# One layer's modulation loads after the projections, the other layer's delta rule projected first

## The chip, the cores and the metric

The kernel runs on one core of one Trainium2 chip. The metric is the device time of one execution in microseconds (us), lower is better. A core has a matrix engine (PE, with its weight loads PEld), a vector engine (DVE), a scalar engine (ACT), GpSimd (POOL) and a sync engine (SP); each takes its instructions in order from its own queue. In this kernel every DMA is issued from SP's queue, so an issue that waits holds up all issues behind it.

## The reference

Two layers work on 512 latent tokens and 256 context tokens of width 1024, in f32. In each layer:

```python
mod_l = split(silu(c) @ mod_w[i] + mod_b[i], 6)      # shifts, scales and gates; mod_c the same from c_ctx
h_l = modulate(x, norm_mix_g[i], mod_l[0], mod_l[1])
pa_l, pb_l, pc_l, pd_l = _cumsplit(h_l @ w_in[i], MIXER_IN)
oa = rwkv7_mixer(pa_l, pa_c, ...)            # delta rule, recurrent, both directions
ob = diff_attention_mixer(pb_l, pb_c, ...)   # softmax attention, two maps
oc = gla_mixer(pc_l, pc_c, ...)              # gated linear attention, chunks of 64
od = gqa_mixer(pd_l, pd_c, ...)              # softmax attention
x = x + mod_l[2] * (concatenate([oa, ob, oc, od]) @ w_out[i])
x = x + mod_l[5] * conv_ffn(modulate(x, norm_ffn_g[i], mod_l[3], mod_l[4]), ...)
```

The second layer computes outputs for the latent tokens alone. Parts 0 and 1 of the modulation are wanted before the projections, part 2 first in the output projection, parts 3 and 4 in the second norm.

## The kernel before

Each layer has a mixing stage and then a feed-forward stage. The mixing stage is written as generators that `weave` interleaves by costs that they yield: `rwkv` (the delta rule), `gla`, `attentions` (the differential attention in two halves and then the grouped-query one), `projections`, and in the first layer `mod_mix`. That order of writing, tile reuse and a reordering at build time fix each engine's queue before the run.

`projections` multiplies the normed tokens by blocks of `w_in`: `win_feat` (L754) gives features by tokens, `win_tok` (L762) tokens by features in tiles of 128 tokens, 24 matmuls each (L770). `weights` (L367) loads a block, ACT casts it to a high part (L382) and POOL subtracts to get the low part (L383). Before the change the order of blocks in both layers is: GLA's q, k, v, r; the delta rule's k, v, r, w, a, g; the differential attention's k, v, q; the grouped-query kv and q. Three flags release the other streams: "gla ready", "rw g" and so on, "da ready" and "gq ready".

The delta rule then computes for each direction `features` (L1417, with L1424 on PE and L1443 on DVE), `blocks` (L1465 on PE, which reads L1443's result), the `bonus` (L1547, which reads L1454 of POOL), and `inverses`: 31 steps of two DVE instructions (L1492 and L1494), each step reading the one before. After the inverses come, chunk by chunk, `rw_prep` (L1620 on PE) and `rw_chain` (L1738, L1743). The attention first prepares its keys (`rope`, then `split_stack` with L937 on DVE, then PE transposes at L432), then runs scores (L1012), a maximum (L1018, DVE), an exponential (L1020, ACT) and values.

`mod_first` computes eight pairs of modulation blocks before the first norm. `mod_mix` (L521) computes the other twelve of the first layer beside the mixing stage: per pair 1 MB of weights, eight small matmuls (L470), a copy (L472, ACT), two matmuls that wait for that copy (L474), and an add (L477). It takes one of PSUM banks 0 to 3, which the projections and the attention use too. The second layer's modulation runs on DVE in the feed-forward stage and is not touched.

Of the kernel before, what the change touches and what calls it, by code (L numbers as in the profile page):

```python
# [15 lines left out]
AF = mybir.ActivationFunctionType  # L16
ALU = mybir.AluOpType
# [4 lines left out]
P = 128  # L22
# [201 lines left out]
class Net:  # L224
# [7 lines left out]
    RB = ((4, 8), (4, 8))  # L232

# [287 lines left out]
    def mod_mix(self, dt):  # L521

        ws = [self.new([4, 256]) for _ in range(3)]
        e = 0
        for i in range(KD, len(MODP)):
            w = []
            for q in range(2):
                self.nc.sync.dma_start(out=ws[e % 3], in_=self.A["modp"][i][:, 4 * q:4 * q + 4])
                w += [ws[e % 3][:, k] for k in range(4)]
                e += 1  # L530
            ps = yield from self.bank(1, 0, 4)
            self.mod_pair(i, w, ps)
            self.free(ps)
            yield dt
        self.free(*ws, self.c32)
# [240 lines left out]
    def projections(self, li, h, S):  # L776
# [6 lines left out]
        h2 = [[a[:, e] for a in h] for e in range(2)]  # L783

        G = S["gla"] = {"q": self.new([T]), "k": self.new([T])}
        yield from self.win_feat(li, "glaq", qs, h2, lambda ps: nc.scalar.mul(out=G["q"][:, :nq], in_=ps[:, :nq], mul=32 ** -0.5), 8)
        yield from self.win_feat(li, "glak", both, h2, lambda ps: nc.scalar.copy(out=G["k"], in_=ps[:, :T]), 8)
        G["v"], G["g"] = self.new([NT, 256]), self.new([NT, 32])

        def ev(t, ps):  # L790
            nc.scalar.copy(out=G["v"][:, t], in_=ps[:, :256])
            nc.vector.tensor_copy(out=G["g"][:, t], in_=ps[:, 256:288])

        yield from self.win_tok(li, "glav", range(NT), h2, ev)
        G["r"] = self.new([NT, 256])

        def evr(t, ps):
            th = self.new([256])
            nc.scalar.activation(out=th, in_=ps[:, :256], func=AF.Tanh, scale=0.5)
            nc.vector.scalar_tensor_tensor(out=G["r"][:, t], in0=th, scalar=1.0, in1=ps[:, :256], op0=ALU.add, op1=ALU.mult)  # L800
            self.free(th)

        yield from self.win_tok(li, "glar", qt, h2, evr)
        S["gla ready"] = True

        R = S["rw"] = {}
        c0 = self.small([P, 9], "c0")
        nc.vector.tensor_tensor(out=c0, in0=self.par(li, "mu0", 0, 9), in1=self.par(li, "mu1", 0, 9), op=ALU.add)
        nc.vector.tensor_scalar(out=c0, in0=c0, scalar1=-1.0, scalar2=1.0, op0=ALU.mult, op1=ALU.add)

        def shifted(i, dst, segs):
            def f(ps):
                n = segs[-1][1]
                nc.scalar.activation(out=dst[:, :n], in_=ps[:, :n], func=AF.Copy, scale=c0[:, i:i + 1])
                for a, b in segs:
                    nc.vector.scalar_tensor_tensor(out=dst[:, a + 1:b], in0=ps[:, a:b - 1], scalar=self.par(li, "mu0", i),
                                                   in1=dst[:, a + 1:b], op0=ALU.mult, op1=ALU.add)
                    nc.vector.scalar_tensor_tensor(out=dst[:, a:b - 1], in0=ps[:, a + 1:b], scalar=self.par(li, "mu1", i),
                                                   in1=dst[:, a:b - 1], op0=ALU.mult, op1=ALU.add)
            return f  # L820

        for nm, i0, m, segs in (("k", 2, 2, both), ("v", 4, 2, both), ("r", 0, 2, qs), ("w", 6, 1, both), ("a", 7, 1, both), ("g", 8, 1, qs)):
# [1123 lines left out]
```

## Time and profile before

| | us |
|---|---|
| runs | 2373.57, 2382.31, 2385.05 (median 2382.31) |
| profiled execution | 2371.69, of which the span is 2369.8 |
| PE busy in the span | 2194.0 (93%) |
| first layer: projections, then the rest of its mixing stage | 64 to 391, 391 to 743 |
| second layer: mixing stage | 1392 to 1960 |

The profiled execution is 10.6 us below the median of the runs. Stretches are given in us from the start of the span; their bounds were chosen at the first norm's end, the end of the first layer's projections, the start of the output projection, and in the second layer where PE's idle share changes.

### The profile page before, as it was taken

How to read it: one execution, taken by the hardware profiler on the slowest of the kernel's cores; microseconds unless marked ns; L12 is line 12 of the kernel's file. 1: busy time of each engine (PE TensorE's matmuls, PEld its weight loads, DVE VectorE, ACT ScalarE, POOL GpSimd, SP SyncE). 2: the span in 40 equal slices, each digit the busy share in tenths (PEclk: the TensorE clock that was granted, in tenths of full speed). 3: DMA queues.
4: the chain of work that ended last, by engine and by line, in shares of the span. 5: the costliest groups of instructions: out<-in, count | busy, mean ns of one | idle time of the engine just before them, and what ended most of it. 6: DMA issues, size and time to landing. Idle time of an engine off the chain costs nothing. (4 is left out here: it accounts for less than half of the span.)

```text
span 2369.8 us, 40603 instructions
## 1 busy us (share of the span) xinstructions
PE 2194.0 (93%) x15656; PEld 1852.1 (78%) x15656; DVE 1327.0 (56%) x2900; ACT 934.2 (39%) x1730; POOL 995.9 (42%) x999
## 2 busy tenths in 40 slices
PE   7989996889989999999999989995899979999999
PEld 3877786768768788888888877785778868888888
DVE  3143567878864696765445643378877565332323
ACT  3333222555564422322223443332465544433333
POOL 1433437123422344434434634455443224555556
PEclk7999997889999999999999989997889989999999
DMA  8322354433234243343333521144233242333334
GB/s 324 116 72 82 102 150 108 105 89 93 58 123 143 82 137 116 109 142 106 116 107 107 172 65 55 59 126 132 69 98 87 77 138 72 102 94 99 98 98 134
DMA packets 241265, 258.51 MB, mean 109 GB/s; under 512 B 102896, under 2 KB 186160, under 8 KB 241072
## 3 DMA queue, kind: packets, MB, share of 16 engines
q1 hardware_dynamic: 241072, 255.92, 36.1%
q8 instruction: 123, 2.02, 0.4%
q14 instruction: 70, 0.57, 0.1%
HBM read 209.69 MB, written 37.77 MB: 104 GB/s over the span
## 5 line engine op out<-in xcount | busy, mean ns | idle before, releaser
L392 PE MATMUL pst<-slab,slab 128*128 128x512 f32 (+1 forms) x6552 | 1236.5, 350 | 14.4 <-POOL slab L650 5.8
L392 PEld LDWEIGHTS pst<-slab,slab 128*128 128x128 f32 x6552 | 1049.6, 190 | 195.8 <-issue 11.3
L383 POOL TENSOR_TENSOR slab<-slab,slab 128x512 fp32r<-128x512 f32 (+1 forms) x428 | 563.7, 1326 | 661.1 <-ACT slab L382 621.3
L382 ACT CAST slab<-slab 128x512 fp32r<-128x512 f32 (+1 forms) x428 | 258.7, 612 | 592.3 <-PE pst L392 418.6
L770 PE MATMUL pst<-slab,slab 128*128 128x256 f32 (+1 forms) x1872 | 254.1, 295 | 9.3 <-POOL slab L383 8.0
L770 PEld LDWEIGHTS pst<-slab,slab 128*128 128x128 f32 x1872 | 242.4, 199 | 20.4 <-POOL slab L383 9.5
L432 PE MATMUL pst<-cst,slab 128*128 128x128 f32 (+1 forms) x968 | 166.4, 305 | 69.1 <-DVE slab L937 21.7
L683 DVE SCALAR_TENSOR_TENSOR slab<-pst,pp,slab 128x511 f32<-128x511 f32 x66 | 41.6, 658 | 299.2 <-ACT slab L680 299.2
L432 PEld LDWEIGHTS pst<-cst,slab 128*128 128x128 f32 (+1 forms) x968 | 120.6, 153 | 96.6 <-DVE slab L937 24.3
L1620 PE MATMUL pst<-slab,slab 128*128 128x128 f32 (+4 forms) x1320 | 160.8, 283 | 7.3 <-DVE slab L1646 3.4
L1620 PEld LDWEIGHTS pst<-slab,slab 128*128 128x128 f32 (+3 forms) x1320 | 132.3, 179 | 29.6 <-issue 14.6
L714 DVE SCALAR_TENSOR_TENSOR slab<-pst,fgate,slab 128x512 f32<-128x512 f32 (+1 forms) x144 | 88.2, 628 | 104.9 <-PE pst L392 104.7
L1020 ACT ACTIVATE slab<-pst,mx 128x768 f32<-128x768 f32 (+1 forms) x120 | 97.7, 815 | 67.6 <-DVE mx L1018 64.3
L1018 DVE TENSOR_REDUCE mx<-pst 128x1 f32<-128x768 f32 (+1 forms) x120 | 100.2, 846 | 35.6 <-PE pst L1012 20.1
L695 POOL TENSOR_TENSOR slab<-slab,slab 128x768 fp32r<-128x768 f32 (+1 forms) x44 | 73.9, 1680 | 70.2 <-ACT slab L694 70.2
L551 DVE SCALAR_TENSOR_TENSOR slab<-slab,slab 128x512 bf16<-128x512 f32 x104 | 92.2, 886 | 5.1 <-DMA slab<-in_modw_dram 3.5
L1048 PE MATMUL pst<-slab,slab 128*64 128x128 f32 x832 | 67.0, 290 | 5.0 <-DVE slab L429 2.9
L1031 ACT ACTIVATE slab<-slab,r 128x768 f32<-128x768 f32 (+1 forms) x80 | 67.7, 852 | 10.0 <-DVE r L1030 9.3
L689 ACT ACTIVATE slab<-slab 128x768 f32<-128x768 f32 (+1 forms) x44 | 32.4, 737 | 85.7 <-DVE slab L685 85.6
L694 ACT CAST slab<-slab 128x768 fp32r<-128x768 f32 (+1 forms) x44 | 32.1, 729 | 85.0 <-DVE slab L691 84.9
L1012 PE MATMUL pst<-slab,slab 128*128 128x384 f32 (+1 forms) x144 | 48.8, 407 | 14.0 <-ACT slab L1020 6.4
L1048 PEld LDWEIGHTS pst<-slab,slab 128*64 128x64 f32 x832 | 46.9, 141 | 18.1 <-DVE slab L429 6.3
(320 smaller groups left out, 2626.6 us busy)
## 6 DMA issues: line engine op xcount, KB each, us to landing
slab<-in_wup_dram SPq DMA_DIRECT2D x88, 512.0 KB, 3.7
slab<-in_modw_dram SPq DMA_DIRECT2D x112, 256.0 KB, 3.0
slab<-in_wdn_dram SPq DMA_DIRECT2D x48, 512.0 KB, 3.5
slab<-in_win_dram SPq DMA_DIRECT2D x46, 512.0 KB, 3.9
slab<-in_modp_dram SPq DMA_DIRECT2D x40, 512.0 KB, 7.0
slab<-in_wout_dram SPq DMA_DIRECT2D x16, 512.0 KB, 3.7
slab<-in_xT_dram SPq DMA_DIRECT2D x16, 384.0 KB, 5.3
slab<-kb SPq DMA_DIRECT2D x24, 256.0 KB, 3.0
```

The source lines that it names most:

```text
L382: nc.scalar.copy(out=w[0], in_=st[:, k:k + q])
L383: nc.gpsimd.tensor_tensor(out=w[1], in0=st[:, k:k + q], in1=w[0].bitcast(F32), op=ALU.subtract)
L392: self.nc.tensor.matmul(ps[:, a:b], w[i][k][:, cols], x[j][k][:, a:b], start=(k == 0 and q == 0), stop=(k == nk - 1 and q == 2))
L432: self.nc.tensor.transpose(out, a.bitcast(F32) if a.dtype != F32 else a, self.c["ident"])
L551: self.tc.keep_in_program_order(nc.vector.scalar_tensor_tensor(out=junk, in0=w, scalar=1.0, in1=self.sc[s][e], op0=ALU.mult, op1=ALU.mult, ...
L695: nc.gpsimd.tensor_tensor(out=HL[:, 1, :n], in0=th[:, :n], in1=HL[:, 0, :n].bitcast(F32), op=ALU.subtract)
L714: nc.vector.scalar_tensor_tensor(out=x[m][:, a:b], in0=ps[:, a:b], scalar=gate[:, m, s:s + 1], in1=x[m][:, a:b], op0=ALU.mult, op1=ALU.add)
L770: self.nc.tensor.matmul(ps[:, :n], h[i][k][:, t * P:(t + 1) * P], w[j][k], start=(k == 0 and q == 0), stop=(k == KD - 1 and q == 2))
L1018: nc.vector.tensor_reduce(out=mx, in_=sv, axis=AX.XY, op=ALU.max, negate=True)
L1020: nc.scalar.activation(out=p[m][:, a:].rearrange("p (e c) -> p e c", e=2 - a // hb), in_=sv, func=AF.Exp, bias=mx, accum_out=lsum[:, m:m + 1])
L1048: nc.tensor.matmul(acc[64 * e:64 * e + 64, :P], vs[e][:, i + j], aT[:, 256 * j + P * e:256 * j + P * e + P], start=(first and j == 0), sto ...
L1620: mm = lambda o, a, b, pos: nc.tensor.matmul(o, a, b, start=True, stop=True, tile_position=pos)
```

## The change

Three edits, with everything they pull along through the interleaving:

- `mod_mix` first waits for "gq ready", the last flag of the first layer's projections. Its loads are 48 of 256 KB instead of 24 of 512 KB, into twelve tiles instead of three, and the pairs are yielded every 4000 instead of 16000 cost units.
- In the second layer (`DELTA = (1,)`) the delta rule's blocks are projected before GLA's. In both layers its w and a now come before r and g; `rwkv` waits for all of them before its features.
- The first attention begins when six slabs of the arena are free instead of five.

```diff
+    DELTA = (1,)
-    def mod_mix(self, dt):
-        ws = [self.new([4, 256]) for _ in range(3)]
-        e = 0
+    def mod_mix(self, S, dt):
+        n = 12
+        yield from self.wait(S, "gq ready")
+        ws = [self.new([2, 256]) for _ in range(n)]
         for i in range(KD, len(MODP)):
             w = []
-            for q in range(2):
-                self.nc.sync.dma_start(out=ws[e % 3], in_=self.A["modp"][i][:, 4 * q:4 * q + 4])
-                w += [ws[e % 3][:, k] for k in range(4)]
-                e += 1
+            for q in range(4):
+                t = ws[(4 * i + q) % n]
+                self.nc.sync.dma_start(out=t, in_=self.A["modp"][i][:, 2 * q:2 * q + 2])
+                w += [t[:, k] for k in range(2)]
...
+        def gla(hi):
             G = S["gla"] = {"q": self.new([T]), "k": self.new([T])}
...
+        def delta(hi):
             R = S["rw"] = {}
...
-        for nm, i0, m, segs in (("k", 2, 2, both), ("v", 4, 2, both), ("r", 0, 2, qs), ("w", 6, 1, both), ("a", 7, 1, both), ("g", 8, 1, qs)):
+            for nm, i0, m, segs in (("k", 2, 2, both), ("v", 4, 2, both), ("w", 6, 1, both), ("a", 7, 1, both), ("r", 0, 2, qs), ("g", 8, 1, qs)):
...
+        for i, f in enumerate((delta, gla) if li in self.DELTA else (gla, delta)):
+            yield from f(4 if i else 8)
...
             if before is None:
-                yield from self.room(5)
+                yield from self.room(6)
...
-                streams.append(self.mod_mix(16000))
+                streams.append(self.mod_mix(S, 4000))
```

The counts of instructions are the same on every engine but for the 24 additional loads. What moves is shown at three places. Lines behind the edited functions stand 2 to 7 higher in the changed file: L1492 and L1494 of before are L1499 and L1501 there, L937 is L944, L770 is L773, L1547 is L1554, L1706 is L1713, L1508 to L1510 are L1515 to L1517.

On DVE in the second layer, where the first key is split (L937) among the last inverse steps. Before:

```order
L920 TENSOR_TENSOR slab_322_6989<-slab_322_6989,slab_340_11497 128x128
L1494 TENSOR_TENSOR slab_355_12059<-slab_355_12059,slab_353_11875 96x5x27
L412 SCALAR_TENSOR_TENSOR rs0qda_13664<-rs1qda_13665,rs0qda_13664 128x32
L924 TENSOR_TENSOR slab_322_6989<-slab_322_6989,rs0kda_13154 128x128
L1492 TENSOR_TENSOR slab_353_11875<-slab_353_11875,slab_355_12059 96x112
L920 TENSOR_TENSOR slab_21_169<-slab_21_169 128x128
L1494 TENSOR_TENSOR slab_355_12059<-slab_355_12059,slab_353_11875 96x4x28
L937 TENSOR_TENSOR slab_390_13745<-slab_322_6989,slab_390_13745 128x8x32
```

The changed kernel on the same engine, at the last inverse step of the layer (GLA's gate L1215 to L1231 and the query norms follow it):

```order
L1501 TENSOR_TENSOR slab_18_166<-slab_18_166,slab_373_12000 96x2x30
L1499 TENSOR_TENSOR slab_373_12000<-slab_373_12000,slab_18_166 96x31
L1501 TENSOR_TENSOR slab_18_166<-slab_18_166,slab_373_12000 96x31
L863 TENSOR_REDUCE msqda_13460<-slab_21_169 128x8
L1215 TENSOR_SCALAR slab_33_385<-pst,pp 128x768
L1219 SCALAR_TENSOR_TENSOR slab_118_3789<-reset,slab_33_385 128x768
L863 TENSOR_REDUCE msqda_13460<-slab_368_11840 128x8
L1231 TENSOR_TENSOR slab_324_7081<-slab_118_3789 128x768
```

Counted over the whole queue: before, 34 of the layer's 62 inverse steps stand behind the first key's split and 25 behind the first maximum of the scores; now none does, and the first split stands 75 rows behind the last step.

On PE in the second layer, at the end of the bonus. Before, the keys' transposes follow at once:

```order
L1547 MATMUL pst<-rk_12898,slab_151_4601 128x2
L1547 MATMUL pst<-rk_12898,slab_94_3573 128x2
L432 MATMUL pst<-cst,slab_390_13745 128x128 x12
L770 MATMUL pst<-slab_212_5540,slab_315_6605 128x256
L770 MATMUL pst<-slab_329_7170,slab_315_6605 128x256
```

The changed kernel at the same place:

```order
L1554 MATMUL pst<-rk_12209,slab_382_12218 128x2
L1554 MATMUL pst<-rk_12209,slab_324_7081 128x2
L773 MATMUL pst<-slab_330_7192,slab_334_7209 128x256
L773 MATMUL pst<-slab_331_7196,slab_334_7209 128x256
L773 MATMUL pst<-slab_330_7192,slab_334_7209 128x256
```

Behind the bonus 216 projection matmuls were left before, and 576 are now; when the first score is issued 168 were left, and now none is. In the first layer it is the other way round: none was left behind the first score or the first L1620, and now 142 and 48 are.

On SP in the first layer, where the delta rule's exchanges are issued (L1508 and L1509 load chunks, L1687 and L1706 copy between partitions). Before:

```order
L1505 DMA slab_22_170<-ra_91 128x512
L1508 DMA slab_18_166<-scrout_389 64x4x64
L1706 DMA slab_18_166<-slab_5_100 64x64 x7
L1687 DMA slab_98_3637<-slab_98_3637 64x4x128 x2
L1706 DMA slab_18_166<-slab_5_100 64x64
```

The changed kernel, with the pairs' loads (L532) between the chunk loads and the copies (L1713 and L1694):

```order
L1515 DMA slab_23_171<-scrout_392 64x4x64 x3
L532 DMA slab_16_164<-in_modp_dram 128x512
L532 DMA slab_96_3437<-in_modp_dram 128x512 x2
L976 DMA slab_33_385<-rawdaq 128x128
L532 DMA slab_22_170<-in_modp_dram 128x512
L532 DMA slab_6_101<-in_modp_dram 128x512 x3
L532 DMA slab_7_102<-in_modp_dram 128x512
L1713 DMA slab_22_170<-slab_96_3437 64x64 x4
L532 DMA slab_7_102<-in_modp_dram 128x512 x2
L532 DMA slab_16_164<-in_modp_dram 128x512
L1694 DMA slab_118_3789<-slab_112_3742 64x4x128 x2
```

The 24 loads of `mod_mix` stood among the loads of the projection weights; now 48 stand among these exchanges.

## Rows read from the trace of the kernel before

**Rows 1.** The page: span, busy share of PE, its 40 slices, the granted clock.

```profile
span 2369.8 us, 40603 instructions
...
PE 2194.0 (93%) x15656; PEld 1852.1 (78%) x15656; DVE 1327.0 (56%) x2900; ACT 934.2 (39%) x1730; POOL 995.9 (42%) x999
...
PE   7989996889989999999999989995899979999999
...
PEclk7999997889999999999999989997889989999999
```

**Rows 2.** Stretches: bounds, length, busy us and instructions by engine, clock, DMA.

```profile
core 0: us, PE busy (x) PEld busy (x) DVE busy (x) ACT busy (x) POOL busy (x), PEclk, DMA share, GB/s
64.00:391.00 327.00, 300.85 (x2542) 258.23 (x2541) 147.43 (x335) 99.34 (x176) 137.78 (x138) 0.96 0.35 107
391.00:500.00 109.00, 83.19 (x640) 66.94 (x639) 84.86 (x204) 48.87 (x101) 37.35 (x65) 0.76 0.38 95
500.00:743.00 243.00, 226.86 (x2147) 185.33 (x2148) 179.02 (x476) 145.48 (x318) 73.29 (x115) 0.97 0.37 106
1392.00:1594.00 202.00, 191.22 (x1590) 164.42 (x1588) 94.22 (x187) 76.01 (x130) 95.22 (x84) 0.98 0.27 75
1594.00:1657.00 63.00, 38.15 (x320) 34.31 (x318) 50.58 (x139) 14.77 (x32) 32.83 (x47) 0.78 0.51 140
1657.00:1740.00 83.00, 67.32 (x494) 57.55 (x496) 71.99 (x178) 43.46 (x86) 33.49 (x57) 0.88 0.31 82
1740.00:1924.00 184.00, 178.34 (x1870) 150.68 (x1868) 121.66 (x292) 110.52 (x232) 62.15 (x98) 0.97 0.35 93
1924.00:1960.00 36.00, 23.08 (x164) 18.55 (x161) 16.93 (x58) 10.66 (x20) 6.20 (x7) 0.81 0.36 116
```

**Rows 3.** PE's waits in 1594 to 1740: total us, times, longest.

```profile
PE pst L1465 <- DVE slab L1443: 10.1, 1, 10.1
PE pst L432 <- DVE slab L937: 7.8, 3, 7.1
PE pst L1547 <- POOL slab L1454: 3.1, 1, 3.1
```

**Rows 4.** DVE's queue around L1443 at 1619: start, us, instruction.

```profile
1619.39 0.41 DVE L1492 TENSOR_TENSOR slab<-slab,slab 96x247 f32<-96x247 f32 x1
1619.71 0.95 DVE L1443 TENSOR_TENSOR slab<-slab,slab 128x768 f32<-128x768 f32 x1
1620.58 0.40 DVE L1494 TENSOR_TENSOR slab<-slab,slab 96x247 f32<-96x247 f32 x1
```

**Rows 5.** Stretch 1594 to 1740, L1492 and then L1494 alone: DVE busy.

```profile
1594.00:1740.00 146.00, 26.05 (x62) 0.84 0.40 107
...
1594.00:1740.00 146.00, 25.43 (x62) 0.84 0.40 107
```

**Rows 6.** PE's waits in 64 to 391.

```profile
PE pst L474 <- ACT slab L472: 7.2, 2, 4.3
```

**Rows 7.** PE's waits in 391 to 743.

```profile
PE pst L432 <- DVE slab L937: 13.6, 6, 4.9
```

**Rows 8.** The page: costliest groups, the projections by tokens.

```profile
L770 PE MATMUL pst<-slab,slab 128*128 128x256 f32 (+1 forms) x1872 | 254.1, 295 | 9.3 <-POOL slab L383 8.0
```

**Rows 9.** L1018, first layer and second: durations, first and last start.

```profile
L1018 DVE TENSOR_REDUCE mx<-pst x72: 405/948/959, 419.9 to 719.2; 128x1 f32<-128x768 f32 x48, 128x1 f32<-128x256 f32 x24
...
L1018 DVE TENSOR_REDUCE mx<-pst x48: 939/957/959, 1657.8 to 1925.9; 128x1 f32<-128x768 f32 x48
```

**Rows 10.** Stretch 64 to 391, L470 and then L474 alone: PE, PEld busy.

```profile
64.00:391.00 327.00, 13.61 (x176) 4.92 (x176) 0.96 0.35 107
...
64.00:391.00 327.00, 7.05 (x44) 6.74 (x44) 0.96 0.35 107
```

**Rows 11.** L528 in 64 to 391: issue time in ns, then landing.

```profile
L528 SPq DMA_DIRECT2D slab<-in_modp_dram x19: 327/382/1103, 74.0 to 329.6; - x19
...
DMA to landing us min/median/max: 3.7/5.1/7.4
```

**Rows 12.** The page: DMA issues, size of one, median us to landing.

```profile
slab<-in_modw_dram SPq DMA_DIRECT2D x112, 256.0 KB, 3.0
slab<-in_wdn_dram SPq DMA_DIRECT2D x48, 512.0 KB, 3.5
```

More of the change, by code (lines that the diff above doesn't have):

```diff
@@ L783, in projections @@
         h2 = [[a[:, e] for a in h] for e in range(2)]
[L785 to L820, printed above, removed]
@@ L822, in projections, with ev, evr @@
-        for nm, i0, m, segs in (("k", 2, 2, both), ("v", 4, 2, both), ("r", 0, 2, qs), ("w", 6, 1, both), ("a", 7, 1, both), ("g", 8, 1, qs)):
-            R[nm] = [self.new([T]) for _ in range(m)]
-            for p in range(m):
-                yield from self.win_feat(li, f"rw{i0 + p}", segs, h2, shifted(i0 + p, R[nm][p], segs))
-            S["rw " + nm] = True
+        def gla(hi):
+            G = S["gla"] = {"q": self.new([T]), "k": self.new([T])}
+            yield from self.win_feat(li, "glaq", qs, h2, lambda ps: nc.scalar.mul(out=G["q"][:, :nq], in_=ps[:, :nq], mul=32 ** -0.5), hi)
+            yield from self.win_feat(li, "glak", both, h2, lambda ps: nc.scalar.copy(out=G["k"], in_=ps[:, :T]), hi)
+            G["v"], G["g"] = self.new([NT, 256]), self.new([NT, 32])
+            def ev(t, ps):
+                nc.scalar.copy(out=G["v"][:, t], in_=ps[:, :256])
+                nc.vector.tensor_copy(out=G["g"][:, t], in_=ps[:, 256:288])
+            yield from self.win_tok(li, "glav", range(NT), h2, ev)
+            G["r"] = self.new([NT, 256])
+            def evr(t, ps):
+                th = self.new([256])
+                nc.scalar.activation(out=th, in_=ps[:, :256], func=AF.Tanh, scale=0.5)
+                nc.vector.scalar_tensor_tensor(out=G["r"][:, t], in0=th, scalar=1.0, in1=ps[:, :256], op0=ALU.add, op1=ALU.mult)
+                self.free(th)
+            yield from self.win_tok(li, "glar", qt, h2, evr)
+            S["gla ready"] = True
@@ new lines, in delta, with shifted, f @@
+        def delta(hi):
+            R = S["rw"] = {}
+            c0 = self.small([P, 9], "c0")
+            nc.vector.tensor_tensor(out=c0, in0=self.par(li, "mu0", 0, 9), in1=self.par(li, "mu1", 0, 9), op=ALU.add)
+            nc.vector.tensor_scalar(out=c0, in0=c0, scalar1=-1.0, scalar2=1.0, op0=ALU.mult, op1=ALU.add)
+            def shifted(i, dst, segs):
+                def f(ps):
+                    n = segs[-1][1]
+                    nc.scalar.activation(out=dst[:, :n], in_=ps[:, :n], func=AF.Copy, scale=c0[:, i:i + 1])
+                    for a, b in segs:
+                        nc.vector.scalar_tensor_tensor(out=dst[:, a + 1:b], in0=ps[:, a:b - 1], scalar=self.par(li, "mu0", i),
+                                                       in1=dst[:, a + 1:b], op0=ALU.mult, op1=ALU.add)
+                        nc.vector.scalar_tensor_tensor(out=dst[:, a:b - 1], in0=ps[:, a + 1:b], scalar=self.par(li, "mu1", i),
+                                                       in1=dst[:, a:b - 1], op0=ALU.mult, op1=ALU.add)
+                return f
+            for nm, i0, m, segs in (("k", 2, 2, both), ("v", 4, 2, both), ("w", 6, 1, both), ("a", 7, 1, both), ("r", 0, 2, qs), ("g", 8, 1, qs)):
+                R[nm] = [self.new([T]) for _ in range(m)]
+                for p in range(m):
+                    yield from self.win_feat(li, f"rw{i0 + p}", segs, h2, shifted(i0 + p, R[nm][p], segs), hi if nm == "k" else 4)
+                S["rw " + nm] = True
```

## The prediction

> **What bounds the kernel now.** I read the page first. PE is busy for 2194.0 of 2369.8 us, so the whole kernel can lose at most 176 us of idle time to a better order; PE's slices and the clock's dip at the same places, in the two mixing stages [rows 1]. I then cut those stages into stretches [rows 2]. In the second layer PE is busy 94.7% of 1392 to 1594 and 96.9% of 1740 to 1924, but 105.5 of the 146 us between (38.15 + 67.32 in 63 + 83): 40.5 us are idle there. DVE is the busiest engine in the first of the two pieces, 50.58 of 63 us. PE's waits say why: 10.1 us for L1443, 7.8 us for the first keys' L937, 3.1 us for L1454 [rows 3]. L1443 stands between inverse steps in DVE's queue [rows 4], and those steps take 26.05 + 25.43 = 51.5 us of DVE in this stretch alone [rows 5]. So DVE's long serial loop collides with the second direction's features and with the attention's first keys, while PE has little else queued. In the first layer PE is busy 300.9 of 327 us during the projections (26 idle), 83.2 of 109 behind them (26 idle), 226.9 of 243 after that (16 idle) [rows 2]. The pairs of `mod_mix` lie in the first of these, and the waits for the first keys in the second [rows 6, 7].
>
> **The second layer, part by part.** The new order issues the same instructions, so its worth is in the 40.5 idle us. All 62 inverse steps now stand ahead of the first key's split, and 576 instead of 216 projection matmuls stand behind the bonus. At 254.1/1872 = 0.136 us each [rows 8], 576 are 78 us of PE work, which covers the loop's 51.5 us of DVE. If the 105.5 us of PE work goes through at the 94.7% of the stretch ahead of it, it takes 111 us: -35. The lowest is 0 (the idle time stays), the highest the whole 40.5.
>
> The clock comes on top. It was 0.78 over 63 us and 0.88 over 83 us, against 0.98 ahead [rows 2]: at its two levels (2.4 and 1.2 GHz) that is 0.20x2x63 + 0.10x2x83 = 42 us more at half clock, of which PE was busy 72%, 30 us. Work bound by columns would win 15 of these; small matmuls that wait for weights win less, so I take 8 (bounds 0 and 15). The Trainium skill, "TensorE: Matmul & The Clock Gate", part "What's actually happening", says that the array is throttled by default and that activity releases it; by that alone all 15 would come back, and the sum below would be 7 us lower. The stretch's rows show the clock falling with PE's idle share, but not how much of the work follows it.
>
> Against this stands what the new order cannot cover. The chain from features to blocks is the same length and now has the inverses of the first direction in it still; the keys still need ACT, POOL and DVE before PE can transpose. Of the 21 us of waits named above I leave a third, +7 (bounds 0 and 21). Projecting GLA later costs nothing as long as it ends before the output projection; its cover is the attention, which lasts from 1657 to 1926 [rows 9]. The order of w, a, r and g costs nothing, because the delta rule waits for all of them anyway. Six free slabs instead of five act through the queue's order alone. Second layer: -35 - 8 + 7 = -36.
>
> **The first layer.** The pairs cost PE 13.61 + 7.05 us in the projections' stretch [rows 10], for 11 of the 12, and PE waits 7.2 us for the copy between their two steps [rows 6]. All of this, 28 us, leaves a stretch that PE bounds: -28. The work itself comes back behind it: 20.7x12/11 = 22.5 us. There 42 us of PE are idle (25.8 + 16.1), and half of the work should fall into them: +11 (bounds 0 and 22.5). The copy's wait returns in part: +4 (0 to 10). The first keys' waits of 13.6 us [rows 7] now have projection matmuls between them, 142 behind the first score, 19 us of work: -9 (0 to -13.6). Sum -22. On SP 24 loads become 48; one issue took 0.38 us at the median [rows 11], so 24 more are some 9 us of a queue that is not the bound. The loads bring 12.6 MB into a stretch whose DMA engines are busy 37 to 38% [rows 2]; what that costs is the slower rival below, and 0 in this sum, since they are issued ahead by up to three pairs.
>
> **Sum.** -36 - 22 = -58 against the profiled execution's 2371.7: 2314. That execution was 10.6 us below the median of the runs, 2382.3; the same 58 us off the median gives 2324, and I say 2325. By the bounds the second layer lies between +7 and -55 and the first between +4 and -42; both at the same end are not expected, and for this case alone I give 2295 to 2360. A measurement tells about 0.5%, 12 us, from no change.
>
> **The rivals.** *The attention sets the second layer's end.* Its maxima run from 1657.8 to 1925.9, 268 us [rows 9], and now start behind the last projection matmul. That puts 168 x 0.136 = 23 us more PE work ahead of the first score, as much as the 25 us that PE idles in 1594 to 1657 [rows 2]: the start stays, and if the attention again needs 268 us the stage ends where it did. Then only the first layer gains: 2382 - 22 = 2360. For it: the attention is one serial stream. Against: in the first layer the same stream did 72 maxima in 299 us, 4.2 us each against 5.6 here [rows 9], so it can run faster when PE lets it. Chance 0.15.
>
> *The waits only move.* In the second layer the blocks still wait for L1443, which still stands behind inverse steps, and GLA's chain, now woven into the token projections, waits in the keys' place; in the first layer the 22.5 us of pairs and their 7.2 us of waits come back whole, because the stretch they go to is bound by chains across engines, and every added matmul lengthens one. Both layers then gain nothing: 2382, within 12. For it: DVE was at 78% there too (84.86 of 109) [rows 2]. Chance 0.14.
>
> *The pairs' loads stand in the way of the delta rule.* This is the slower side. SP issues in order, and 16 loads of 256 KB now stand between the chunk loads and the copies that a chunk's PE steps wait for. One such load lands in 3.0 us [rows 12]; if the four of a pair hold up the exchange behind them one after another, that is 12 us for each of 12 pairs, 144 us. With half to two thirds of the pairs in front of an exchange that PE waits for, 72 to 96 us, the time would be 2382 - 58 + 72 = 2396 to 2420. It decides from 58/12 = 4.8 us per pair. For it: the pairs' own loads of 512 KB took 5.1 us at the median beside the projections [rows 11]. Against: the DMA engines moved only 95 GB/s there [rows 2], and a load of 512 KB from another tensor lands in 3.5 us [rows 12], hardly longer than one of half the size, so loads overlap. The Trainium skill, "DMA: Bandwidth & Descriptors", part "Bandwidth", has the rule to batch loads to 1 MiB, and the fit in its part "Anatomy of one DMA" (2.0 us and 436 KB per us, for DMAs issued from POOL) makes a pair 4x2.6 instead of 2x3.2 us if loads go one by one, an estimate of 48 us over 12 pairs; the rows here agree that half a load is far from half as long (3.0 and 3.5 us). Chance 0.13.
>
> **How the numbers follow.** The forecast case keeps 0.58. Faster by over 0.5%: 0.58, and most of the attention's case (0.13) = 0.71. Same: 0.02 of it, 0.12 of the moved waits, and 0.02 of the loads' case = 0.16. Slower: 0.13. The range leaves out the slower rival and the edges: 2292, for a clock and cover at their bounds, to 2376, which takes in the attention's case.
>
> **What would show it.** Right: in the second layer PE busy over 93% in every stretch from the norm to the attention's end, no wait for L1443 (now L1450) above 3 us, the inverses' last step 50 us or more ahead of the first maximum; the output projection 532 instead of 568 us behind the stage's start. In the first layer the projections end near 360, their stretch has no small matmuls, and the next is no longer than before. Wrong: PE waiting for L1713, L1694 or L1515's landings in the first layer; a clock under 0.8 over 50 us or more in the second; or attention maxima that again take 268 us while PE idles.

## The result: slower by 1%

The changed kernel takes 2402.67 us (median of 4 runs, 2396.89 to 2404.17), the kernel before 2378.44 in the runs beside it (2373.57 to 2385.05): ratio 1.0098, 95% interval 1.0073 to 1.0123. The forecast was 2325. The page of the changed kernel (span, PE's busy share, its slices, the granted clock; answers to [rows 1]):

```profile
span 2395.1 us, 40626 instructions
...
PE 2210.8 (92%) x15656; PEld 1859.4 (78%) x15656; DVE 1332.4 (56%) x2900; ACT 935.8 (39%) x1730; POOL 1001.1 (42%) x999
...
PE   6999868899899999999999989788699989999999
...
PEclk8999978799999999999999989879799999999999
```

The span grew by 25.3 us: 16.8 of them are more PE busy time for the same 15656 instructions, 8.5 more idle time. Two marks divide the growth, the moments at which DVE reaches the first product of each output projection (L1822 before, L1829 after). Before they stand at 734.8 and 1956.2 us, now at 748.6 and 1979.8: the first layer's mixing lost 13.8 us, and from the first mark to the second the time went from 1221.4 to 1231.2, +9.8. Neither layer gained. The stretches of the changed kernel follow, in the columns of [rows 2]: the first layer's projections, two pieces behind them, then the second layer's mixing stage.

```profile
61.00:404.00 343.00, 300.76 (x2491) 263.83 (x2490) 179.56 (x397) 113.04 (x200) 158.18 (x164) 0.92 0.30 86
404.00:520.00 116.00, 102.31 (x880) 75.08 (x877) 67.55 (x196) 48.47 (x112) 23.69 (x47) 0.84 0.56 163
520.00:757.00 237.00, 214.58 (x1986) 173.66 (x1986) 160.84 (x428) 133.97 (x286) 69.77 (x108) 0.94 0.36 101
1405.00:1530.00 125.00, 119.35 (x800) 100.82 (x799) 67.73 (x115) 50.13 (x84) 55.76 (x47) 0.97 0.41 113
1530.00:1610.00 80.00, 59.51 (x520) 52.67 (x518) 57.52 (x141) 19.32 (x36) 40.62 (x36) 0.75 0.29 77
1610.00:1697.00 87.00, 79.24 (x758) 70.88 (x756) 32.73 (x95) 21.26 (x41) 38.54 (x49) 0.95 0.24 70
1697.00:1740.00 43.00, 25.80 (x168) 20.30 (x167) 33.49 (x89) 18.78 (x38) 23.02 (x48) 0.68 0.31 89
1740.00:1960.00 220.00, 205.15 (x2046) 168.64 (x2045) 162.79 (x390) 131.88 (x272) 69.56 (x113) 0.98 0.31 83
```

The first layer's projections end at 404 instead of 386 us, although eleven pairs have left them: PE is busy as long as before (300.76 against 300.85 us) and idles 42 instead of 26 us. Other work stands in the pairs' place, 169 instructions of it (2491 against 2542 less the pairs' 220), and the clock is 0.92 instead of 0.96. PE's waits there (61 to 404; L1472, L1554 and L944 are before's L1465, L1547 and L937):

```profile
PE pst L1472 <- DVE slab L1450: 12.9, 1, 12.9
PE pst L773 <- POOL slab L385: 7.2, 4, 5.9
PE pst L1554 <- POOL slab L1461: 6.6, 1, 6.6
PE pst L434 <- DVE slab L944: 5.5, 1, 5.5
```

The first, the third and the fourth are the three waits of [rows 3], the second layer's collision of the inverses with the second direction's features and with the first keys, now in the first layer. In the second layer, where the change was to remove them, they are gone from 1405 to 1697, and others stand there; a second group follows behind the last projection (1697 to 1984):

```profile
PE pst L773 <- POOL slab L385: 10.2, 3, 6.4
PE pst L1284 <- DVE slab L1276: 6.9, 1, 6.9
PE pst L1273 <- POOL slab L1268: 4.4, 4, 1.7
PE pst L1209 <- DVE slab L1201: 3.8, 1, 3.8
...
PE pst L434 <- DVE slab L944: 12.8, 4, 6.0
```

L385 makes the weights' low parts; L1209, L1273 and L1284 are GLA's. As forecast, the last inverse step ends well ahead of the first maximum, at 1625 us. The attention's maxima (L1025, DVE; [rows 9]) start when the projections are over, and the last lies 17 us ahead of the second mark:

```profile
L1025 DVE TENSOR_REDUCE mx<-pst x48: 936/958/958, 1718.4 to 1962.3; 128x1 f32<-128x768 f32 x48
```

### The profile page after: what moved, and what is told of

It reads as the page before. It is cut to its first block, busy times and chain, and to the rows that moved or that the text cites. A ratio compares the mean times of both kernels' runs of the same rounds, so it can differ in the third digit from the quotient of the medians.

```text
span 2395.1 us, 40626 instructions
## 1 busy us (share of the span) xinstructions
PE 2210.8 (92%) x15656; PEld 1859.4 (78%) x15656; DVE 1332.4 (56%) x2900; ACT 935.8 (39%) x1730; POOL 1001.1 (42%) x999
## 5 line engine op out<-in xcount | busy, mean ns | idle before, releaser
L385 POOL TENSOR_TENSOR slab<-slab,slab 128x512 fp32r<-128x512 f32 (+1 forms) x428 | 567.7, 1335 | 652.3 <-ACT slab L384 635.3
L773 PE MATMUL pst<-slab,slab 128*128 128x256 f32 (+1 forms) x1872 | 259.8, 298 | 22.2 <-POOL slab L385 17.4
L773 PEld LDWEIGHTS pst<-slab,slab 128*128 128x128 f32 x1872 | 245.5, 200 | 35.4 <-POOL slab L385 19.6
L1627 PEld LDWEIGHTS pst<-slab,slab 128*128 128x128 f32 (+3 forms) x1344 | 134.6, 176 | 29.7 <-issue 13.6
L554 DVE SCALAR_TENSOR_TENSOR slab<-slab,slab 128x512 bf16<-128x512 f32 x156 | 143.4, 919 | 6.5 <-DMA slab<-in_modw_dram 4.1
L1025 DVE TENSOR_REDUCE mx<-pst 128x1 f32<-128x768 f32 (+1 forms) x120 | 100.4, 846 | 40.1 <-PE pst L1019 25.5
L1659 POOL TENSOR_TENSOR slab<-slab,pc 128x256 f32<-128x256 f32 x48 | 31.4, 670 | 98.3 <-PE pst L1750 27.3
```

The lines of the kernel that those rows point to most:

```text
L385: nc.gpsimd.tensor_tensor(out=w[1], in0=st[:, k:k + q], in1=w[0].bitcast(F32), op=ALU.subtract)
L554: self.tc.keep_in_program_order(nc.vector.scalar_tensor_tensor(out=junk, in0=w, scalar=1.0, in1=self.sc[s][e], op0=ALU.mult, op1=ALU.mult, ...
L773: self.nc.tensor.matmul(ps[:, :n], h[i][k][:, t * P:(t + 1) * P], w[j][k], start=(k == 0 and q == 0), stop=(k == KD - 1 and q == 2))
L1025: nc.vector.tensor_reduce(out=mx, in_=sv, axis=AX.XY, op=ALU.max, negate=True)
L1627: mm = lambda o, a, b, pos: nc.tensor.matmul(o, a, b, start=True, stop=True, tile_position=pos)
```

## The experiments

The table gives for each run the median (us), its ratio to the kernel before on the same chip with the 95% interval, and from one profile the end of the first layer's token projections, the first mark, and the time from mark to mark ("second"), which holds the first layer's feed-forward stage too. A profiled execution lies up to 11 us from the median of its runs, and where mark and median differ both are said. Runs whose first layer is the same put their first marks close together: 734.8, 732.2 and 733.0 (before, e3, e18), 748.6 and 746.6 (changed, e4). So a difference of 3 us between marks says nothing.

One thing holds for the whole table. The reordering at build time places each engine's instructions anew after every edit, also those that the edit does not name. Counted by line and shape ahead of the first mark, 233 of DVE's 1087 instructions stand more than five places elsewhere in e1 than before, 187 in e8 and none in e7; against e5 it is 243 in e16, 219 in e11, 227 in e14, 127 in e13 and 80 in e15. What a run shows is therefore the edit together with the order of queues that it brings.

| run | us | ratio | proj. end | mark 1 | second |
|---|---|---|---|---|---|
| before | 2374 to 2376 | | 386 | 734.8 | 1221.4 |
| changed | 2402.7 | 1.0098 (1.0073–1.0123) | 404 | 748.6 | 1231.2 |
| e1 w, a first | 2399.0 | 1.0104 (1.0087–1.0121) | 393 | 749.4 | 1233.3 |
| e2 pairs moved | 2398.2 | 1.0090 (1.0070–1.0111) | 396 | 740.8 | 1242.9 |
| e3 delta first | 2381.1 | 1.0027 (1.0013–1.0041) | 385 | 732.2 | 1225.7 |
| e4 e1 + e2 | 2406.9 | 1.0137 (1.0117–1.0156) | 401 | 746.6 | 1242.1 |
| e5 e2, tiles held | 2407.9 | 1.0132 (1.0115–1.0150) | 363 | 761.1 | 1231.6 |
| e6 e2, late features | 2429.5 | 1.0238 (1.0224–1.0253) | 373 | 775.4 | 1233.5 |
| e7 a before w | 2375.9 | 1.0008 (0.9993–1.0022) | 386 | 736.4 | 1222.2 |
| e8 r before v | 2392.9 | 1.0084 (1.0063–1.0105) | 390 | 730.9 | 1231.4 |
| e9 e5, no pairs | 2368.9 | 0.9973 (0.9957–0.9988) | 363 | 707.3 | 1237.2 |
| e10 e5, first step | 2407.7 | 1.0141 (1.0113–1.0170) | 361 | 752.7 | 1233.0 |
| e11 e5, one load | 2376.8 | 1.0009 (0.9988–1.0031) | 363 | 731.2 | 1231.0 |
| e12 e5, free adds | 2409.0 | 1.0139 (1.0122–1.0156) | 361 | 760.5 | 1231.3 |
| e13 e5, half bytes | 2387.7 | 1.0064 (1.0039–1.0089) | 361 | 741.4 | 1224.1 |
| e14 e5, 24 loads | 2399.9 | 1.0108 (1.0085–1.0132) | 361 | 746.9 | 1232.6 |
| e15 e5, unread | 2390.2 | 1.0068 (1.0045–1.0091) | 361 | 748.5 | 1225.4 |
| e16 e5, POOL loads | 2376.7 | 1.0005 (0.9986–1.0025) | 364 | 730.3 | 1229.3 |
| e17 changed, POOL loads | 2403.3 | 1.0133 (1.0109–1.0157) | 410 | 759.6 | 1237.3 |
| e18 e3, GLA last | 2442.1 | 1.0287 (1.0273–1.0302) | 386 | 733.0 | 1286.1 |

### The edits one by one (e1 to e4)

e1, on the kernel before:

```diff
-... ("r", 0, 2, qs), ("w", 6, 1, both), ("a", 7, 1, both), ("g", 8, 1, qs) ...
+... ("w", 6, 1, both), ("a", 7, 1, both), ("r", 0, 2, qs), ("g", 8, 1, qs) ...
```

> The kernel before with one edit: w and a projected before r and g in both layers. Theory A (the moved pairs cost the first layer its 14 us, the delta rule ahead of GLA costs the second its 10.6 us): this edit does nothing, 2378 within 6, the first layer's output projection starts at 735 within 4 us, the second layer's stage (first root's end to output projection) lasts 592 within 4. Theory B (the order of w and a brings the features 20 us forward in the first layer, into the second direction's inverses' way, and that is the loss): 2390 to 2402, the first layer's output projection near 749, waits of 10 us and more for L1443 in the first layer.

e2: before with the new `mod_mix` and `self.room(6)`, which its twelve tiles need.

> The kernel before with the pairs of the first layer moved behind the last projection (48 loads, 12 tiles, and six slabs for the attention, which the 12 tiles need), nothing else. Theory A: 2392 within 6, output projection of the first layer near 749, the second layer's stage 592. Theory B: the move alone gains what was forecast of it or part of it: 2356 to 2370, output projection at 713 to 727. A third theory (the loads delay the delta rule's exchange on SP): slower as in A, and PE's waits behind the projections name DMA landings.

e3: before with `DELTA = (1,)` and the two functions that it orders.

> The kernel before with the delta rule projected before GLA in the second layer, nothing else. Theory A: first layer unchanged (735), second layer's stage 592 + 10 = 602, time 2389 within 6. Theory B (the loss of the second layer came with the order of w and a, too): stage 570 to 588, time 2357 to 2374.

e4: the changed kernel with `DELTA = ()`.

> The changed kernel with GLA again projected first in the second layer (the pairs moved, w and a ahead of r and g, six slabs). Theory A: first layer as in the changed kernel (749), second layer's stage 592, time 2392 within 6. Theory B: second layer's stage 600 or more, because w and a stand ahead of r and g there too, time 2400.

Neither theory holds alone. The order of w and a costs 24 us by itself, 14.6 at the first mark and 12 behind it, though it adds no work: behind the projections PE waits once 10.3 us for a key's split (L937) and once 8.4 us for POOL's L1652. Moving the pairs costs as much: 6 us in the first layer, where the waits of the changed kernel stand too (e2's projections; lines one higher than before's):

```profile
PE pst L1466 <- DVE slab L1444: 13.2, 1, 13.2
PE pst L1548 <- POOL slab L1455: 8.4, 1, 8.4
```

and 21.5 us behind it, in stages that the pairs do not run in. Of these some 19 lie in the second layer's mixing stage, where e2 also has the six free slabs; no run has those alone. The costs do not add: 1.04% and 0.90% alone make 1.37% together (e4). The delta rule first costs 0.27% by itself (e3) and takes some 0.4% back on top of the other two (0.98% for the changed kernel; the two intervals overlap by a little).

e3 shows why it gains nothing. The second layer from the first norm's last root to the mark, before (first three rows) and e3 (as [rows 2]):

```profile
1364.00:1440.00 76.00, 65.80 (x405) 57.13 (x404) 29.74 (x83) 29.14 (x58) 30.38 (x30) 0.91 0.25 73
1440.00:1697.00 257.00, 211.68 (x1758) 180.12 (x1756) 171.39 (x389) 92.82 (x163) 120.23 (x133) 0.91 0.32 89
1697.00:1956.00 259.00, 235.31 (x2323) 198.51 (x2322) 173.46 (x434) 143.04 (x294) 84.39 (x134) 0.94 0.36 98
```

```profile
1362.00:1440.00 78.00, 67.51 (x353) 55.33 (x353) 41.55 (x107) 31.77 (x53) 28.31 (x23) 0.89 0.25 76
1440.00:1697.00 257.00, 222.27 (x1822) 193.01 (x1820) 152.09 (x347) 79.51 (x149) 120.42 (x136) 0.86 0.33 88
1697.00:1958.00 261.00, 237.26 (x2302) 195.80 (x2303) 186.70 (x449) 153.57 (x312) 84.24 (x138) 0.95 0.34 95
```

PE idles 69 instead of 79 us (596 - 527.0, 592 - 512.8), so the waits did shrink; but the same work is busy 14 us longer. The clocks of the rows put 91 us of before's 592 at the lower level, 1.2 GHz, and 115 us of e3's 596 (2 x 0.09 x 76 for the first row, and so on). In the traces PE is busy for 62 us at that level before and for 85 in e3; if half of the 23 us more was lost, that is 12 of the 14 us, an estimate. Over these stretches the 864 token matmuls alone, before and then in e3, are busy 7.5 us longer:

```profile
1364.00:1956.00 592.00, 118.53 (x864) 113.44 (x864) 0.92 0.33 91
...
1362.00:1958.00 596.00, 126.06 (x864) 118.42 (x864) 0.90 0.32 89
```

Of those with 256 columns 50 lie wholly at the lower level before and 93 in e3, where one takes 431 to 434 ns on average, against 286 at the upper one. That leaves 596 against 592 us, and 6.7 us by the medians.

### Tile space, and other orders (e5 to e8)

In the trace of e2 240 of the 1008 token matmuls of the first layer start behind the second direction's last features matmul, before only 24. `front` waits for free slabs before it computes features; the pairs' three old tiles lay in them.

e5, on e2:

```diff
+        hold = [self.new([4, 256]) for _ in range(3)]
         yield from self.wait(S, "gq ready")
+        self.free(*hold)
         ws = [self.new([2, 256]) for _ in range(n)]
```

> The pairs moved as in e2, but with the old three tiles of the pairs (12 KB of each partition) kept taken, unused, until the last projection; w, a, r, g and the layers' order as before. Theory A: what cost the first layer was tile space. The second direction's features wait for free slabs; without the pairs' tiles those came free 216 projection matmuls sooner, and the features met the first direction's inverses on DVE (waits of 13.2 and 8.4 us for L1444 and L1455 in e2). Then with the tiles held the features end behind 375, no such wait is over 4 us, and the first layer's output projection starts at 720 to 733 (the gain forecast of the move, or a part of it). Theory B: the pairs were the filler that covered the collision, and their work comes back whole in any place: 735 to 745. The second layer is not part of the test; its order shifts with the tile space too, between 592 and 614 us.

e6, on e2: `ROOM` of the first layer `((14, 4), 7, 4, 2)` instead of `((9, 2), 7, 4, 2)`.

> The pairs moved as in e2, no tiles held, but the second direction's features of the first layer wait for more free space (14 halves and 4 whole slabs instead of 9 and 2), which puts all of them behind the last projection, with the first attention's scores 120 matmuls ahead of the projections' end. Theory A (the early features cost it): no wait for L1444 or L1455 over 4 us in the first layer, output projection at 725 to 738, better than e2's 741. Theory B (the delta rule's chain then starts too late and the stage ends with it): rw_chain ends behind 700 and the output projection starts at 745 or later.

What tile space does was foreseen rightly: with 12 KB held and unused, again 24 token matmuls stand behind the features, the longest of these waits in e5's projections is 1.5 us, and the projections end at 363, 23 us sooner than before, which is the pairs' work.

```profile
PE pst L1468 <- DVE slab L1446: 1.5, 1, 1.5
```

What it is worth was not: mark 1 is 26 us later than before, and 20 us later than in e2, which has the collision and is 10 us faster by the medians. The colliding inverses of the first layer end at 439 us in e2 and at 479 in e5. So the collision's waits are not shown to be a loss by themselves; what e5 loses lies behind the projections (next part). Later still is worse: e6's `rw_chain` ends at 717 us and mark 1 comes at 775, as its second theory said.

e7 and e8, on the kernel before, change places in the same list: a and w; v and r.

> The kernel before with a projected before w, in both layers: two blocks of the same size change places, and no work, tile or wait changes otherwise. If the 14.6 and 12 us that w and a ahead of r cost in e1 come from what that order does to the delta rule, this does nothing: 2374 within 6. If any regrouping of the queues behind the projections costs about that much, because the order before happened to fit: 2384 to 2400.

> The kernel before with r projected before v (k, r, v, w, a, g), in both layers; w, a and g stay last. The delta rule transposes v before its features, so these start as late as before. If e1's cost belongs to w and a standing ahead of r: 2374 within 8. If any regrouping costs: 2384 to 2400, with the extra time again in single waits for DVE's key splits and POOL's products between 370 and 430 and between 1630 and 1720.

Two blocks that enter the same step can change places freely (e7), but this moved nothing in DVE's queue of the first layer and four instructions in ACT's. r ahead of v costs 19 us by the medians (e8, whose runs spread from 2385 to 2403); its profile, 8 us under that median, has no new wait longer than 10 us to put it down to. So the cost is not one that only w and a have, and e8 came where the second theory put it: a regrouping of the queues can cost about that much. Whether every one does, and which dependence makes the cost, is not settled.

### What of the pairs costs (e9 to e12)

All on e5. e9 leaves out loads, matmuls and copies; the other edits:

```diff
 # e10: no second step
-            self.mod_pair(i, w, ps)
+            self.pair_mm(w, ps)            # the eight matmuls
             self.free(ps)
+            self.pair_add(i, None)         # writes the bias
 # e11: loads of the first pair only
-                t = ws[(4 * i + q) % n]
-                self.nc.sync.dma_start(...)
+                t = ws[q]
+                if i == KD:
+                    self.nc.sync.dma_start(...)
 # e12: both steps, the add reads the bias alone
+            self.pair_mm(w, ps)
+            self.pair_sel(self.pair_copy(ps), ps)
             self.free(ps)
+            self.pair_add(i, None)
```

> e5 without the pairs' work: no loads, no matmuls, no copy; the adds write the bias alone, so parts 1 to 5 of the first layer's modulation lack their matrix product. Where e5's first layer lost its 26 us against before although its projections ended 23 us sooner, the pairs must be the cause, or the new interleaving as such is. If the pairs: the output projection at 705 to 720. If the interleaving: 740 or later.

> e5 with the pairs' loads and first step (eight matmuls) alone: no copy, no second matmuls, and adds that write the bias alone. Theory C (the chain from PE over ACT back to PE and on to DVE holds up queues that work in order): most of the loss is gone, output projection at 715 to 735. Theory D (the matmuls' own time, 26.5 us at the half clock) or theory L (the loads): 745 or later.

> e5 with the loads of one pair alone; the other eleven multiply with the same weights, so their parts of the modulation are those of another block. All matmuls, copies and adds stay, 44 of 48 loads go. Theory L (traffic and SP's queue): output projection at 715 to 740. Theories C and D: 755 within 8, and DVE still waits 15 us or more for L474's results.

> e5 with loads, both steps of matmuls and the copy, but adds that write the bias alone and so wait for nothing. Theory C in its narrow form (DVE, which sets this stretch, stands still 23 us for the pairs' results): 735 to 745, DVE's waits for the pairs gone. If the chain on PE and ACT is what counts: 750 or later.

The loads are it, with the order of queues that they bring: without 44 of them the kernel is 30 us faster (e5 against e11, marks and medians alike). Without any pairs mark 1 comes to 707, 27.5 us sooner than before, close to the 28 of the forecast; by the medians, with the longer way to the second mark taken off in the same manner, it is 23. The pairs' own work puts back 24 by the marks (e11 against e9). But e9's profile lies 8 us under its median and e11's 6 over; the medians are 8 us apart, to which the 6 us belong by which e9's way from mark to mark is longer: 14. So it is 14 to 24. Neither the chain of copy and second step (e10) nor DVE's wait for it (e12) has a part that the medians show, though DVE waits 23.2 us for L474 in e5: idle time of an engine that has nothing else ready. From 363 to 540 PE gets 1120 instructions done in e5 and 1419 in e11 (e5 first):

```profile
363.00:540.00 177.00, 142.87 (x1120) 101.17 (x1117) 105.92 (x259) 66.92 (x150) 48.68 (x84) 0.78 0.49 137
```

```profile
363.00:540.00 177.00, 155.85 (x1419) 119.81 (x1419) 129.55 (x325) 87.69 (x195) 65.89 (x112) 0.86 0.37 91
```

### How the loads cost (e13 to e16)

All on e5. e13 loads 128 KB and uses each block of weights twice; e14 loads 24 times 512 KB into six tiles; e15 lets pairs 2 to 12 multiply with the first one's weights and their 44 loads go to tiles that nobody reads; e16:

```diff
-                self.nc.sync.dma_start(out=t, in_=self.A["modp"][i][:, 2 * q:2 * q + 2])
+                self.nc.gpsimd.dma_start(out=t, in_=self.A["modp"][i][:, 2 * q:2 * q + 2])
```

> e5 with the same 48 loads and the same waits, but 128 KB each instead of 256: every second block of weights is left out and its neighbour used twice. If traffic is the cost: half of the 30 us comes back, 2393 within 6, first layer's output projection near 746. If SP's queue (issues or waits): 2408 within 6, near 761.

> e5 with 24 loads of 512 KB into six tiles: the same bytes in the same space, half the issues. If the number of issues is the cost: 2393 within 6, output projection near 746. If traffic or the wait for tiles: 2408 within 6.

> e5 with all 48 loads, of which only the first pair's are read (the other pairs multiply with the same weights); the other 44 go to tiles that PE never reads, so that SP waits for no matmul before it issues one. If the wait for tiles holds up SP: 2377 to 2387, output projection at 731 to 740. If traffic or the number of issues: 2408 within 6.

> e5 with the 48 loads issued by POOL instead of SP, the same bytes, tiles and reads. If SP's queue is what suffers (issues or waits): 2377 to 2390, output projection at 731 to 743, unless POOL's own work behind the loads suffers in its place (then POOL's queue shows the wait). If traffic: 2408 within 6.

The loads' traffic is not the cost: with the same bytes issued by POOL the whole 31 us is back. That leaves SP's queue, or the order of the other queues that comes with it: e16 changes both, and no run changes one of them alone. Nor is a single cause left inside SP's queue. Half the bytes give back 20 us (e13, the time that its expectation gave to traffic), no wait for tiles 18 (e15, between its two expectations), half the issues 8 (e14, the same), each by the medians. The 18 cannot be that wait alone, since SP stands only some 6 us at these loads in e5, mostly in two places:

```profile
SPq L532 <- DVE slab L940: 3.5, 1, 3.5
...
SPq L532 <- PE pst L432: 1.9, 2, 1.6
```

SP's queue in e5 shows what stands in line (start, us, instruction):

```profile
479.73 2.49 SPq L532 DMA_DIRECT2D slab<-in_modp_dram  x2
482.32 0.37 SPq L1506 DMA_DIRECT2D slab<-kb  x1
485.22 0.33 SPq L1508 DMA_DIRECT2D slab<-ra  x1
485.64 0.61 SPq L1511 DMA_DIRECT2D slab<-scrout  x1
486.29 0.61 SPq L1512 DMA_DIRECT2D slab<-scrin  x1
...
495.31 2.04 SPq L532 DMA_DIRECT2D slab<-in_modp_dram  x4
```

A chunk of the delta rule is loaded by six copies (kb, ra, and twice scrout and scrin) of 0.33 to 0.61 us of SP's time each, in order behind pairs' loads of 0.43 at the median. In 363 to 520 the counts and landings in e5 and then in e16 are:

```profile
slab<-in_modp_dram SPq DMA_DIRECT2D x42, 256.0 KB, 4.3
...
slab<-scrout SPq DMA_DIRECT2D x11, 64.0 KB, 3.1
```

```profile
slab<-in_modp_dram POOLq DMA_DIRECT2D x42, 256.0 KB, 4.8
...
slab<-scrout SPq DMA_DIRECT2D x16, 64.0 KB, 2.7
```

In the same 157 us 11 instead of 16 of the chunks' copies are issued. Once issued they land about as fast: scrout 3.1 against 2.7 us, but scrin 3.5 against 4.8. So the engines that move the data are not what e5 loses by, nor is the DMA queue that SP's loads share with these copies (in e16 the loads have one of their own). The Trainium skill, "DMA: Bandwidth & Descriptors", part "Issuing engines are not separate DMA queues", says that issuing from several engines saves only the sequencer's time, usually little. An issue here is small beside its DMA too (0.43 against 4.3 us). But 42 of them are 42 x 0.43 = 18 us of a queue that the chunks wait for, 24 with the 6 us of waiting, and the runs show 31.

### The changed kernel and the second layer once more (e17, e18)

e17: e16's edit on the changed kernel. e18, on e3: `gla` is projected behind the attention's blocks in the second layer.

> The changed kernel with the 48 loads of the pairs issued by POOL instead of SP. If SP's queue is the main cost of the first layer there too: its output projection comes forward from 749 to 720 to 735, and the whole takes 2374 to 2390. If the collision of the early features with the inverses (25 us of waits at 332 to 364) is the main cost: 743 or later, 2395 or more; those waits stay in either case.

> e3 (the kernel before with the delta rule first in the second layer) with GLA's blocks projected last there, behind the attention's, instead of between the two. If the late start of the attention ends the second layer in e3 (from 1686 to 1951): the attention starts some 30 us sooner, and the stage falls from 596 to 565 to 585 us, 2350 to 2370. If PE's lower clock and the chains between the stretches set it: 592 or more, 2376 or more; then GLA's own chain, now last, may end the stage.

e17 gives nothing back: 2403.3 against 2402.7. POOL now stands 20.3 us at these loads for tiles, longer than the 11.4 in e16 (POOL's waits behind the projections, e17 and then e16):

```profile
POOL slab L532 <- PE pst L472: 20.3, 7, 7.1
```

```profile
POOL slab L532 <- PE pst L470: 11.4, 2, 7.2
```

So SP's queue is not shown to be the price in the changed kernel. What differs there in the first layer is the early features and the order of w and a: with loads on POOL mark 1 is 730.3 without them (e16) and 759.6 with them (e17, profiled 11 us above its median). So with the loads on POOL both together cost 18 to 29 us. With the loads on SP the early features gain 20 (e2 against e5), and the order costs some 6 to 8 by the marks (e2 against e4 and the changed kernel). So the parts have no price of their own. Of the runs with moved pairs and the whole work only e16, with late features and with the loads off SP, brings mark 1 ahead of before's, by 4.5 us. No run took the collision alone out of the changed kernel, and its share there stays open.

e18 does not shorten the stage by an earlier attention. The scores begin 116 us sooner than in e3, at 1570, but the delta rule's chunks begin at 1730 instead of 1684, and the stage ends as before's did (12.9 us there), only later, with PE waiting for the delta rule's output:

```profile
PE pst L434 <- DMA slab<-od: 15.5, 1, 15.5
```

What an earlier attention would gain beside an undelayed delta rule, no run shows.

## Why the prediction was wrong, step by step

Two steps failed, one in each layer. In the first, the loads and the tiles of the moved pairs were put at nothing: the loads alone are worth 30 us where the features stay late (e5 against e11), and the moved pairs made that layer 6 us longer where 22 were to be won (e2). In the second, the new order was to turn 40.5 idle us into work: alone (e3) it took away 10, and PE's busy time, which no bound of the forecast let grow, rose by 14. That layer's part was -36 and measured +6.7 by the medians of e3.

- *The pairs leave the projections, -28.* Right in size: 23 to 27.5 for all of the pairs' work (e9), and 23 at the end of the projections (e5). In the changed kernel the projections end 18 us later instead: the tiles that left with the pairs started the second direction's features 216 matmuls sooner. That the pairs' tiles delayed those features was not seen.
- *Half of the pairs' work falls into idle time, +11, and +4 for the copy.* 14 to 24 against 15 (e9, e11): not refuted, at the low side of what was measured.
- *The loads cost 0; SP's queue "is not the bound".* Failed, by 31 us, where the features stay late (e5, e16). The slower rival named the place, but its sign, PE waiting for landings, did not show, and part of the 31 us can be the new order of the other queues. In the changed kernel the loads' share is not shown (e17), so that its time lies in that rival's 2396 to 2420 is no proof of it.
- *The order of w, a, r and g costs nothing.* Failed: 24 us alone (e1), 6 to 8 of the first layer's on top of the moved pairs.
- *The keys' waits, -9.* They fell from 13.6 us [rows 7] to 9.9 (5.5 ahead of 404 and 4.4 behind), and 19.5 us for L1450 and L1461 (12.9 + 6.6) came in: the new order was costed as if only the keys stood in DVE's queue there. Whether these waits made the first layer longer is not shown, since e5, without them, is slower than e2.
- *The second layer at 94.7% busy, -35, with +7 of waits left.* Failed: the blocks' wait went, the idle time stayed: 76 us in 603, against 79 in 592. It moved to weights, GLA's chain and the keys behind the last projection: the rival of the moved waits, plus a part. The forecast's slow end for this layer, +7, was too low by its own bounds, which give +21 (0, 0 and the whole 21 us of waits).
- *The clock, -8.* Wrong in sign. PE's busy time in that stage rose from 512.8 to 526.9 us (1377 to 1980) on the same instructions, and the 0.75 over 80 us from 1530 is a sign of being wrong that the forecast had named. The Trainium skill's rule that activity releases the clock ("TensorE: Matmul & The Clock Gate", "What's actually happening") agrees with the rows: 0.75 where PE is busy 59.5 of 80 us, 0.68 at 25.8 of 43. PE's busy share of a whole stretch does not give its clock, though: e3's middle row is busier than before's (222.27 against 211.68 us) at a lower clock (0.86 against 0.91). So less idle time did not bring the clock back.
- *The attention sets the end.* Half right: its maxima took 244 us, not 268, and started 47 us later in the stage (60.6 less the first layer's 13.8). They outlast the delta rule now; an earlier start gained nothing in e18, where the delta rule came later.

## What to carry to other kernels

Before work is moved out of a stretch, ask what it holds there besides the engine: here its tiles set when another chain could start, and its loads came among the short copies of a chain in SP's queue. Idle time that a chain makes can move with the chain, and the clock can fall where it goes: count it as gained only when the chain itself gets shorter. And where a build places instructions anew after each edit, an edit's price holds for the order that came with it; prices of single edits did not add here.

## What was not expected

The time from mark to mark is 1221 us before and 1222 in e7, and 1224 or more in every other run, though in e2, e5, e6 and e9 to e16 the code behind the first mark differs in nothing but the six free slabs. Cut at the feed-forward stage's last product it is 633.3 + 588.1 us before. In e2 it is 635.4 + 607.5, so the growth lies in the second layer's mixing stage, where 168 token matmuls start behind the bonus, before 216. In e5, e10 to e13, e15 and e16 it is 638.5 to 642.2 + 585.2 to 593.9, so most of it lies in the first layer's feed-forward stage. These runs share the six slabs, so what sets them apart beyond the spread of executions comes from the first layer, by the order of the queues or by what it leaves in the tile pool; no run separates these, nor the slabs' own part.

A pair's matmul (L470) took 0.403 us at the median over the first layer before and 0.631 in e5. The clock does not explain it: the 228 of e5's that lie wholly at the upper level have the same median of 0.631, against 0.379 for 220 such before. What does is open. And the move had little to win: e9, which leaves the pairs' work of the mixing stage out altogether, is 0.27% faster than before, and no version with the whole work beat before.
